# Measured durations in the forecast that orders the attention's matmuls, and token-reordering copies that run in the order of what they write

## The chip, the cores and the metric

The kernel runs on one core of a Trainium2 chip. The metric is the device time of one execution in microseconds (us), lower is better. Five engines matter here: TensorE (PE in the profile, with PEld for its weight loads), VectorE (DVE), ScalarE (ACT), GpSimd (POOL), and SyncE (SP), which issues most of the DMAs.

## The reference, cut to what matters

Two encoder layers on 512 tokens of width 1024, all in float32. Each layer has two token mixers that share one input projection, then an output projection, a normalisation and an MLP.

```python
for i in range(DEPTH):                                  # DEPTH = 2
    proj = x @ w_in[i]                                  # q, k, v of both mixers and the branch gates
    # mixer A: 8 query heads on 2 key/value heads, |i-j| <= 128, with a sink logit
    oa = banded_attention(rope(qa), rope(ka), va, 128, sink)
    # mixer B: three head groups, (window, dilation) = (128,1), (512,4), (2048,16)
    for g, (window, dil) in enumerate(B_GROUPS):
        outs[g], lse[g] = dilated_attention(rope(qb), rope(kb), vb, window, dil)
    ob = sum(softmax(lse, over groups) * outs)
    h = (sigmoid(gl_a) * (oa @ w_branch_a) + sigmoid(gl_b) * (ob @ w_branch_b)) @ w_out
    x = layer_norm(ALPHA * x + h)
    mlp = square(relu(x @ w_up)) @ w_down
    x = layer_norm(ALPHA * x + mlp + sigmoid(x @ w_ple_gate + b) * (p[i] @ w_ple))
```

## The kernel before, in words

Every float32 product is made of three passes of a rounded format: an operand is split into a high part (a cast on ACT, line 222) and a low part (source minus high part, on DVE, line 223), and TensorE adds high*high, high*low and low*high. Lines 274 to 276 are the three passes of a projection.

The attention of a layer is the part that the change touches. Its work on TensorE is of two kinds. The *filler* is the input projections (`ps_('qb', 0, 1)` and the like: 24 matmuls of 128x512, eight steps of three) and, at the end, the branch product `ya`. They need only the residual and the weights. The *units* are the attention proper: four of mixer A (`unit_a`, pairs of heads, names `sa`, `pta`, `oa`), six of mixer B (`unit_b`, names `sb`, `ptb`, `ob`) and two that combine mixer B's groups (`mix_b`, names `ex`, `ey`, `rs`). A unit of mixer A goes like this:

- scores of query block j into two banks (`sa_i_j`, line 433); DVE adds the mask and takes the maximum (line 426), a small DVE step makes the bias (`nm`, line 487), ACT makes the exponentials (line 422);
- transposes of the exponentials (`pta_i_n`, line 411, n from 0 to 5); ACT casts the high part (`ptha`), DVE subtracts for the low part (`ptla`);
- weighted sums of the values (`oa_i_r`, lines 437 and 438: line 437 needs `ptha`, line 438 needs `ptla`), three of these steps for each head r; ACT and DVE join the halves (lines 442, 443);
- a token scale: ACT widens the reciprocals (`wide`, line 450), TensorE transposes them (`rs`, line 456), DVE multiplies (line 457).

A projection of queries or keys is followed by the rotary step (`rope`): a shuffle on DVE (368), a product on DVE (369), a product on POOL (370), a sum on DVE (371), then the split into `qh` and `ql`. A projection of values is followed by a copy on ACT (`vTvb`, line 387 for dilated groups), transposes (`vtvb`, line 401) and a split (`vvvb`).

For the dilated groups the tokens are put in another order on the way. `natural` and `sigma` are two views of the 512 tokens of a row, with axes a (32), b (4), c (4); a token stands at 16a + 4b + c in the one and at 128c + 32b + a in the other.

The order on TensorE is set by a planner in the kernel. `Forecast` holds a clock `fc.t` of TensorE's time, books spans on ACT, DVE and POOL (`fc.on`), and knows when banks come free. At each turn the planner issues the next step of a live unit if the forecast says that its inputs are there, otherwise one step (three matmuls) of the filler, otherwise it lets 0.05 us of forecast time pass. Two limits hold the filler back: three banks for projections (`mm`), and five sets of queries and keys in use at a time (`held["qk"] - held["free_qk"] < 5`), where a unit gives its sets back when its last scores are issued. `HOP = 0.35` is the forecast's time from one engine to the next.

TensorE then runs in exactly that order (`manual_schedule(engines={PE})`). The order on the other engines is set by the scheduler of the framework, with its own estimates; the forecast does not set it. Weights are prepared two sets ahead: the cast `whi` (ACT, 1024 wide) and the subtraction `wlo` (DVE) of set c+2 take the buffer that set c-1 has left, and so start when a projection's last matmul but one is done.

Of the kernel before, what the change touches and what calls it, by code (L numbers as in the profile page):

```python
# [21 lines left out]
S = 512  # L22
# [177 lines left out]
def build(nc, tc, plan, down, xT, xN, pT, wst, vec, rows, sink, cst, out):  # L200
# [3 lines left out]
    with ctx:  # L204
# [138 lines left out]
        def attention_block(l, av, rp, vt, OA, OB, begun):  # L343
# [11 lines left out]
            def natural(ap):  # L355
                return ap.rearrange("p (a b c) -> p a b c", a=32, b=4)

            def sigma(ap):
                return ap.rearrange("p (c b a) -> p a b c", c=4, b=4)

            def forecast_split(n, after):
                h = fc.on("act", 0.05 + n / 1200, after + HOP)
                return h, fc.on("dve", 0.07 + n / 960, h + HOP)

            def rope(ps, dil, name):
                sw = av.tile([P, S], F32, tag="sw", name="sw" + name, bufs=2)
                t1 = av.tile([P, S], F32, tag="t1", name="t1" + name, bufs=2)
                nc.vector.stream_shuffle(sw, ps, SWAP)
                nc.vector.tensor_tensor(t1, ps, cc["cos"], ALU.mult)
                nc.gpsimd.tensor_tensor(sw, sw, cc["sin"], ALU.mult)  # L370
# [7 lines left out]
                a = fc.on("dve", 0.6, fc.t + HOP)  # L378
                b = fc.on("dve", 0.6, a)
                c = fc.on("pool", 1.23, a + HOP)  # L380
                fc.give("mm", b + HOP)
                return hi, lo, forecast_split(S, fc.on("dve", 0.6, max(b, c) + HOP))[1] + HOP

            def values(ps, kind, name):
                v = av.tile([P, S], F32, tag="vT", name="vT" + name, bufs=2)
                if kind == "sigma":
                    nc.scalar.copy(sigma(v), natural(ps))
# [6 lines left out]
                t = fc.on("act", 0.5, fc.t + HOP) + HOP  # L394
                fc.give("mm", t)
                return v, t

            def values_T(v, name):
                tp = bank("pt", "vt" + name)
                for b in range(4):  # L400
                    nc.tensor.transpose(tp[:, b * P:(b + 1) * P], v[:, b * P:(b + 1) * P], ident)
                vv = av.tile([P, 4, 2, 2, 64], F32R, tag="vv", name="vv" + name, bufs=3)
                split(vv[:, :, :, 0, :], vv[:, :, :, 1, :], tp.rearrange("p (b r d) -> p b r d", b=4, r=2))
                t = forecast_split(S, fc.pe(0.43))[1] + HOP
                fc.take("pt", t)
                return vv, t

            def probs_T(srcs, name):
                tp = bank("pt", "pt" + name)
                for i, s in enumerate(srcs):  # L410
                    nc.tensor.transpose(tp[:, i * P:(i + 1) * P], s, ident)  # L411
# [4 lines left out]
                t = forecast_split(n, fc.pe(n / 1200))[1] + HOP  # L416
                fc.take("pt", t)
                fc.take("pT")
                return hi, lo, t

            def exped(ap, bias, den, n, after):
                nc.scalar.activation(ap, ap, AF.Exp, bias=bias, scale=0.125, accum_out=den)
                return fc.on("act", 0.28 + n / 1200, after) + HOP

            def masked(dst, ps, mask, mx):
                nc.vector.tensor_tensor_reduce(dst, ps, mask, 1.0, NEG, ALU.add, ALU.max, mx)
                return fc.on("dve", 0.07 + mask.shape[-1] / 960, fc.t + HOP)
# [12 lines left out]
            def join(f, o, r):  # L440
                a, b = slice(r * 64, r * 64 + 64), slice(64 - r * 64, P - r * 64)
                nc.scalar.copy(f[a, :], o[b, :])
                nc.vector.tensor_tensor(f[a, :], o[a, :], f[a, :], ALU.add)
                t = fc.on("dve", 0.6, fc.on("act", 0.48, fc.t + HOP) + HOP) + HOP
                fc.give("o", t)
                return t

            def widened(c, name, after):
                wide = av.tile([P, 4, 2, 64], F32, tag="wide", name="wide" + name, bufs=1)
                nc.scalar.copy(wide, c.rearrange("p r (j u) -> p j r u", u=1).to_broadcast([P, 4, 2, 64]))  # L450
                return wide, fc.on("act", 0.52, after) + HOP

            def token_scaled(f, wide, name, after):
# [4 lines left out]
                t = fc.on("dve", 0.6, max(fc.pe(0.43) + HOP, after)) + HOP  # L458
# [7 lines left out]
            def unit_a(i):  # L466
# [9 lines left out]
                for j in range(4):  # L476
# [5 lines left out]
                    fc.pe(6 * w / 2400)  # L482
# [5 lines left out]
                    t = fc.on("dve", 0.08, t + 0.13) + HOP  # L488
# [7 lines left out]
                wide, t_wide = widened(den, nm_, ex[1, 3] + 0.6)  # L496
# [21 lines left out]
                for n, (r, kbs) in enumerate(groups):  # L518
# [8 lines left out]
                    for kb, p in zip(kbs, parts_of(n)):  # L527
                        w = len(p) * P
                        weighted(o[:, p[0][0] * P:p[0][0] * P + w], v, kb, r, pT, slice(c, c + w), kb == 0, kb == 2)
                        fc.pe(2 * w / 2400)  # L530
# [18 lines left out]
            def unit_b(sp, g, st):  # L549
# [4 lines left out]
                if g == 0:  # L554
# [6 lines left out]
                    for jj in range(2):  # L561
# [7 lines left out]
                        fc.pe(1.24)  # L569
# [10 lines left out]
                        t = fc.on("dve", 0.08, t + 0.13) + HOP  # L580
# [3 lines left out]
                else:  # L584
# [3 lines left out]
                    for c in range(4):  # L588
                        cs = slice(c * P, (c + 1) * P)
                        pair_scores(ss, q, k, cs, cs, cs)  # L590
                        fc.pe(0.64)
                    for s in range(2):
# [5 lines left out]
                        t = fc.on("dve", 0.08, t + 0.13) + HOP  # L598
# [27 lines left out]
                for n, (s, ms) in enumerate(groups):  # L626
# [7 lines left out]
                    if ms:  # L634
# [4 lines left out]
                        fc.pe(0.43)  # L639
                        if n % 2:  # L640
                            t_f = join(f, o, s)
                    else:
# [4 lines left out]
                        fc.pe(0.64)  # L647
                        nc.scalar.copy(natural(f[s * 64:s * 64 + 64, :]), sigma(o[:64, :]))
                        t_f = fc.on("act", 0.48, fc.t + HOP) + HOP
# [9 lines left out]
            def mix_b(sp, cn, cs):  # L659
# [11 lines left out]
                t1 = fc.on("dve", 0.6, fc.pe(0.43) + HOP) + HOP  # L671
# [23 lines left out]
                t += 2.6  # L695
# [38 lines left out]
            def steps(key, xs):  # L734
                yield lambda: fc.open("mm")
                w = weights(key)
                fc.on("dve", 1.135, fc.on("act", 0.947, fc.t + HOP) + HOP)
                ps = bank("mm", "ps_" + "_".join(str(v) for v in key))
                fc.take("mm")
                for i, x in enumerate(xs):  # L740
                    mm3(ps, w, i, x, i == 0, i == len(xs) - 1)
                    fc.pe(0.645)
                    yield None
                return ps

            def filler():
# [6 lines left out]
                for kind, *idx in FLOW:  # L753
# [9 lines left out]
                    elif kind == "g":  # L763
                        ps = yield from steps((l, ("g", 0, *idx)), X)
                        ga.append(gate(l, 0, idx[0], vt, rp, ps))
                        fc.give("mm", fc.on("act", 0.57, fc.t + HOP) + HOP)
                    else:
# [3 lines left out]
                        fc.on("dve", 1.135, fc.on("act", 0.947, fc.t + HOP) + HOP)  # L771
                        for n, g in enumerate(ga[2 * u:2 * u + 2]):
# [3 lines left out]
                            for i in range(4):  # L776
                                mm3(ps, w, n * 4 + i, OA[i], i == 0, i == 3)
                                fc.pe(0.645)
                                yield None
                            nc.vector.scalar_tensor_tensor(g, g, 1.0, ps, ALU.add, ALU.mult)  # L780
                            fc.give("mm", fc.on("dve", 0.6, fc.t + HOP) + HOP)
# [551 lines left out]
```

## Time and profile before

| | us |
|---|---|
| median of 3 runs | 1546.28 (1545.49 to 1547.36) |
| the profiled execution, time | 1546.11 |
| the profiled execution, span of its instructions | 1544.3 |
| attention of layer 1, from its first transposes to its last filler | 29.5 to 281.4 |
| attention of layer 2 | 798.0 to 1049.9 |

The profiled execution is 1.8 us longer than its span, and 0.17 us under the median. The mean granted clock of TensorE is 0.997. In the profile's rows a matmul's duration (0.39 us for 128x512) is longer than the step from one to the next (0.23 us), because they are pipelined; the step is what counts. The same holds in part on DVE and ACT: the next instruction starts some 0.05 to 0.1 us before the end that is shown.

### The profile page before, as it was taken

The page shows a single profiled execution, that of the slowest core. Times are in us where ns is not written, and L with a number is a line of the kernel's source. Part 1 is how long each engine was busy: PE and PEld are TensorE (multiplying, and loading weights), DVE is VectorE, ACT ScalarE, POOL GpSimd, SP SyncE. Part 2 cuts the span into 40 slices and gives each one's busy share as a digit, 9 for nine tenths or more (in the row PEclk, how much of TensorE's full clock was granted, in tenths as well). Part 3 has the DMA queues.
Part 4 walks back from the last instruction along what each step waited for, and adds up shares of the span by engine and source line. Part 5 has one row for each costly group of instructions (what it writes and reads, how often), then busy time and mean ns, then how long its engine had stood idle before and what let it go on. Part 6 is the DMA issues. An engine that isn't in the chain of part 4 may idle for free.

```text
span 1544.3 us, 19518 instructions
## 1 busy us (share of the span) xinstructions
PE 1512.5 (98%) x7416; PEld 1241.6 (80%) x7416; DVE 1091.1 (71%) x1809; ACT 714.9 (46%) x1186; POOL 201.3 (13%) x159
## 2 busy tenths in 40 slices
PE   8999999999999999999999999999999999999996
PEld 6778788888888888888887778888888888888885
DVE  6778675457568767696877786744575776767868
ACT  4566554344334443444546665543442443444342
POOL 1111110020011120202010101111100211111021
PEclk9999999999999999999999999999999999999998
DMA  6211224245622415142342121255456233241403
GB/s 219 69 55 56 69 69 167 85 127 161 194 71 81 145 49 161 44 151 68 96 149 68 56 69 56 81 164 148 134 140 207 68 98 121 71 134 55 150 1 95
DMA packets 46317, 162.19 MB, mean 105 GB/s; under 512 B 5648, under 2 KB 5776, under 8 KB 46224
## 3 DMA queue, kind: packets, MB, share of 16 engines
q1 hardware_dynamic: 43200, 152.00, 30.7%
q0 software_dynamic: 2448, 8.91, 3.1%
q8 instruction: 58, 0.95, 0.3%
q14 instruction: 35, 0.29, 0.1%
q10 hardware_dynamic: 576, 0.04, 0.0%
HBM read 155.16 MB, written 4.19 MB: 103 GB/s over the span
## 4 chain that ended last, share of the span: by engine, by line
PE 89%; DVE 6%; ACT 2%; DMA 2%; issue 1%; SPq 0%; ACTq 0%; DVEq 0%
PE dn L1004 17%; PE ps_up L275 8%; PE ps_up L274 8%; PE ps_up L276 8%; PE wo L281 2%; PE wo L282 2%; PE wo L280 2%; PE pg L282 2%; PE pg L281 2%; PE pg L280 2%; DVE wlo L223 1%; PE sa L433 1%; PE sb L433 1%; PE pta L411 1%; PE ps_start L274 1%
## 5 line engine op out<-in xcount | busy, mean ns | idle before, releaser
L223 DVE TENSOR_TENSOR wlo<-wst,whi 128x1024 fp32r<-128x1024 f32 (+1 forms) x171 | 220.2, 1291 | 149.5 <-ACT whi L222 144.8
L222 ACT CAST whi<-wst 128x1024 fp32r<-128x1024 f32 (+1 forms) x171 | 175.5, 1026 | 295.2 <-PE ps_up L275 115.5
L274 PE MATMUL ps_up<-xhi,whi 128*128 128x512 f32 x512 | 199.2, 389 | 0.0
L275 PE MATMUL ps_up<-xlo,whi 128*128 128x512 f32 x512 | 199.2, 389 | 0.0
L276 PE MATMUL ps_up<-xhi,wlo 128*128 128x512 f32 x512 | 199.2, 389 | 0.0
L977 POOL TENSOR_TENSOR hr<-r 128x512 f32<-128x512 f32 x64 | 102.2, 1597 | 551.4 <-ACT r L969 531.0
L274 PEld LDWEIGHTS ps_up<-xhi,whi 128*128 128x128 f32 x512 | 96.1, 188 | 20.0
L276 PEld LDWEIGHTS ps_up<-xhi,wlo 128*128 128x128 f32 x512 | 96.1, 188 | 20.0
L275 PEld LDWEIGHTS ps_up<-xlo,whi 128*128 128x128 f32 x512 | 96.1, 188 | 19.9
L222 ACT CAST whi<-raw 128x1024 fp32r<-128x1024 f32 x56 | 58.0, 1052 | 97.0 <-PE ps_up L275 57.6
L222 ACT CAST dhi<-raw 128x1024 fp32r<-128x1024 f32 x56 | 58.7, 1052 | 81.9 <-PE dn L1004 60.0
L1023 DVE TENSOR_TENSOR y<-y,dn 128x512 f32<-128x512 f32 x96 | 65.1, 682 | 38.7 <-PE dn L1004 38.7
L957 DVE TENSOR_TENSOR raw<-raw,raw 128x1024 f32<-128x1024 f32 x64 | 86.4, 1349 | 0.2
L223 DVE TENSOR_TENSOR wlo<-raw,whi 128x1024 fp32r<-128x1024 f32 x56 | 68.2, 1221 | 14.1 <-ACT whi L222 14.1
L223 DVE TENSOR_TENSOR dlo<-raw,dhi 128x1024 fp32r<-128x1024 f32 x56 | 69.2, 1239 | 5.4 <-ACT dhi L222 5.2
L1004 PE MATMUL dn<-whi,smh 128*128 128x512 f32 x128 | 50.1, 394 | 0.7 <-DVE y L1023 0.7
L282 PE MATMUL pg<-bhi,xlo 128*128 128x512 f32 x128 | 49.9, 390 | 0.9 <-DVE xlo L901 0.9
L1004 PE MATMUL dn<-wlo,smh 128*128 128x512 f32 x128 | 50.6, 395 | 0.2
L1004 PE MATMUL dn<-whi,sml 128*128 128x512 f32 x128 | 49.9, 390 | 0.0
L280 PE MATMUL pg<-bhi,xhi 128*128 128x512 f32 x128 | 49.9, 390 | 0.0
L1004 PE MATMUL dn<-dhi,smh 128*128 128x512 f32 x128 | 49.9, 390 | 0.0
L1004 PE MATMUL dn<-dlo,smh 128*128 128x512 f32 x128 | 49.8, 389 | 0.0
(834 smaller groups left out, 3878.4 us busy)
## 6 DMA issues: line engine op xcount, KB each, us to landing
wst<-wst SPq DMA_DIRECT2D x187, 512.0 KB, 3.6
raw<-wst SPq DMA_DIRECT2D x64, 512.0 KB, 4.3
y<-rows POOLq DMA_DIRECT2D x14, 512.0 KB, 7.8
row<-rows SPq DMA_DIRECT2D x7, 512.0 KB, 9.4
wst<-wst SPq DMA_DIRECT2D x10, 256.0 KB, 3.6
xs<-xT SPq DMA_DIRECT2D x8, 256.0 KB, 5.0
y<-xN SPq DMA_DIRECT2D x4, 512.0 KB, 6.2
kept<-y SPq DMA_DIRECT2D x4, 512.0 KB, 2.8
```

The costliest lines, as they stand in the source:

```text
L222: nc.scalar.copy(hi, src)
L223: nc.vector.tensor_tensor(lo, src, hi.bitcast(F32), ALU.subtract)
L274: nc.tensor.matmul(ps, w[0][:, s], x[0], start=start, stop=False, skip_group_check=part)
L275: nc.tensor.matmul(ps, w[0][:, s], x[1], start=False, stop=False, skip_group_check=part)
L276: nc.tensor.matmul(ps, w[1][:, s], x[0], start=False, stop=stop, skip_group_check=part)
L280: nc.tensor.matmul(ps, x[0], w[0][:, c], start=start, stop=False)
L281: nc.tensor.matmul(ps, x[0], w[1][:, c], start=False, stop=False)
L282: nc.tensor.matmul(ps, x[1], w[0][:, c], start=False, stop=stop)
L957: nc.vector.tensor_tensor(to, to, other, ALU.add)
L977: nc.gpsimd.tensor_tensor(h.rearrange("p s t -> p (s t)"), r, r, ALU.mult)
L1004: nc.tensor.matmul(ps[s], a[:, k, tok], w[b][:, cols], start=first and not (k or m), stop=k == 3 and m == 2, skip_group_check=True)
L1023: return nc.vector.tensor_tensor(to, to, ps, ALU.subtract if n in (2, 4, 5) else ALU.add)
```

## The change

Two things, both in the attention.

First, the durations that the forecast books are changed, nearly all of them upwards: a cast from 0.05 + n/1200 to 0.19 + n/1300, a subtraction from 0.07 + n/960 to 0.15 + n/960, a mask-and-maximum from 0.07 + n/960 to 0.24 + n/960, an exponential from 0.28 to 0.48 + n/1200, the small bias step from 0.08 to 0.2, the preparation of weights from 0.947 and 1.135 to 1.05 and 1.42, a filler step on TensorE from 0.645 to 0.681. Scores of mixer A go from 6w/2400 to 0.35 + 6w/4800; those of mixer B's groups become cheaper (1.24 to 1.1, and 0.64 to 0.45 for each of four).

Second, the copies that put the tokens into the dilated order run through the axes as c, b, a, where they ran as a, b, c. What is written is the same; the writes now go up by one element, and the reads jump by 16 elements, where before the reads went up by one and the writes jumped by 128. This holds for `qh`, `ql` (SBUF to SBUF) and for `vTvb` (PSUM to SBUF).

```diff
-            def sigma(ap):
-                return ap.rearrange("p (c b a) -> p a b c", c=4, b=4)
+            def sigma(ap, order="a b c"):
+                return ap.rearrange(f"p (c b a) -> p {order}", c=4, b=4)
...
             def forecast_split(n, after):
-                h = fc.on("act", 0.05 + n / 1200, after + HOP)
-                return h, fc.on("dve", 0.07 + n / 960, h + HOP)
+                h = fc.on("act", 0.19 + n / 1300, after + HOP)
+                return h, fc.on("dve", 0.15 + n / 960, h + HOP)
...
                 if dil:
-                    split(sigma(hi), sigma(lo), natural(t1))
+                    split(sigma(hi, "c b a"), sigma(lo, "c b a"), natural(t1, "c b a"))
...
                 if kind == "sigma":
-                    nc.scalar.copy(sigma(v), natural(ps))
+                    nc.scalar.copy(sigma(v, "c b a"), natural(ps, "c b a"))
...
-                return fc.on("dve", 0.07 + mask.shape[-1] / 960, fc.t + HOP)
+                return fc.on("dve", 0.24 + mask.shape[-1] / 960, fc.t + HOP)
...
-                    fc.pe(6 * w / 2400)
+                    fc.pe(0.35 + 6 * w / 4800)
...
-                fc.on("dve", 1.135, fc.on("act", 0.947, fc.t + HOP) + HOP)
+                fc.on("dve", 1.42, fc.on("act", 1.05, fc.t + HOP) + HOP)
```

No instruction is added or removed: each engine has as many as before. What moves is the order. On TensorE the units come later against the filler; three places show it, all of layer 1 (layer 2 has the same). In the rows below, the name ahead of the arrow is what is written, the last number of a name is a buffer's.

**Place A**, TensorE, the first unit of mixer A, around the scores `sa_1_2` and the third weighted step of `oa_0_0` (the one that reads `ptha_0_2` and `ptla_0_2`). Before:

```order
L274 MATMUL ps_('qb', 0, 0)_617<-xhi,whi_426 128x512
L275 MATMUL ps_('qb', 0, 0)_617<-xlo,whi_426 128x512
L276 MATMUL ps_('qb', 0, 0)_617<-xhi,wlo_427 128x512
L433 MATMUL sa_1_2_0_621<-qhka_285,qhqa_1_307 128x384
L433 MATMUL sa_1_2_1_622<-qhka_285,qhqa_1_307 128x384
L433 MATMUL sa_1_2_0_621<-qlka_286,qhqa_1_307 128x384
L433 MATMUL sa_1_2_1_622<-qlka_286,qhqa_1_307 128x384
L433 MATMUL sa_1_2_0_621<-qhka_285,qlqa_1_308 128x384
L433 MATMUL sa_1_2_1_622<-qhka_285,qlqa_1_308 128x384
L437 MATMUL oa_0_0_585<-ptha_0_2_595,vvva_322 128x384
L438 MATMUL oa_0_0_585<-ptla_0_2_596,vvva_322 64x384
```

and in the change:

```order
L411 MATMUL pta_0_2_623<-ident,pa_0_0_379 128x128 x3
L433 MATMUL sa_1_2_0_641<-qhka_285,qhqa_1_307 128x384
L433 MATMUL sa_1_2_1_642<-qhka_285,qhqa_1_307 128x384
L433 MATMUL sa_1_2_0_641<-qlka_286,qhqa_1_307 128x384
L433 MATMUL sa_1_2_1_642<-qlka_286,qhqa_1_307 128x384
L433 MATMUL sa_1_2_0_641<-qhka_285,qlqa_1_308 128x384
L433 MATMUL sa_1_2_1_642<-qhka_285,qlqa_1_308 128x384
L437 MATMUL oa_0_0_618<-ptha_0_1_595,vvva_322 128x384
L438 MATMUL oa_0_0_618<-ptla_0_1_596,vvva_322 64x384
L411 MATMUL pta_0_3_656<-ident,pa_0_1_380 128x128 x4
L437 MATMUL oa_0_0_618<-ptha_0_2_627,vvva_322 128x384
```

The projection `ps_('qb', 0, 0)` has moved ahead: it now ends just before this stretch (before, 18 more of its matmuls came behind it), and the next projection is held by the limit on query and key sets until `sa_1_3`. From there to `sa_1_3` no filler stands between the unit's steps.

On DVE the same stretch reads, before:

```order
L426 ISA pa_1_1_408,mxa_1_409<-sa_1_1_1_573,ct_142 128x384
L426 ISA mxa_1_409 128x1
L223 TENSOR_TENSOR wlo_614<-wst_611,whi_613 128x1024
L487 SCALAR_TENSOR_TENSOR nma_1_410<-mxa_1_409,nsk_145 128x2
L223 TENSOR_TENSOR ptla_0_2_595<-pta_0_2_590,ptha_0_2_594 128x384
L223 TENSOR_TENSOR ptla_0_3_606<-pta_0_3_600,ptha_0_3_605 128x512
```

and in the change:

```order
L426 ISA pa_1_1_414,mxa_1_415<-sa_1_1_1_603,ct_142 128x384
L426 ISA mxa_1_415 128x1
L368 STREAM_SHUFFLE sw_qb_0_631<-ps_('qb', 0, 0)_550 128x512
L369 TENSOR_TENSOR t_qb_0_632<-ps_('qb', 0, 0)_550,ct_142 128x512
L223 TENSOR_TENSOR wlo_700<-wst_697,whi_699 128x1024
L487 SCALAR_TENSOR_TENSOR nma_1_416<-mxa_1_415,nsk_145 128x2
L223 TENSOR_TENSOR ptla_0_2_628<-pta_0_2_623,ptha_0_2_627 128x384
```

The rotary step's shuffle and product have come in ahead of `ptla_0_2`, behind the mask step of `sa_1_1`.

**Place B**, TensorE, the third unit of mixer A against the scores `sa_3_2` and `sa_3_3`. Before:

```order
L276 MATMUL ps_('qb', 0, 1)_1020<-xhi,wlo_796 128x512
L437 MATMUL oa_2_0_1054<-ptha_2_1_1044,vvva_322 128x384
L438 MATMUL oa_2_0_1054<-ptla_2_1_1045,vvva_322 64x384
L411 MATMUL pta_2_3_1088<-ident,pa_2_1_747 128x128 x4
L274 MATMUL ps_('qb', 0, 1)_1020<-xhi,whi_795 128x512
L275 MATMUL ps_('qb', 0, 1)_1020<-xlo,whi_795 128x512
L276 MATMUL ps_('qb', 0, 1)_1020<-xhi,wlo_796 128x512
L437 MATMUL oa_2_0_1054<-ptha_2_2_1063,vvva_322 128x384
L438 MATMUL oa_2_0_1054<-ptla_2_2_1064,vvva_322 64x384
L411 MATMUL pta_2_4_1104<-ident,pa_2_1_747 128x128 x3
```

and in the change:

```order
L433 MATMUL sa_3_2_1_1090<-qhka_285,ql_qa_475 128x384
L437 MATMUL oa_2_0_1066<-ptha_2_1_1062,vvva_322 128x384
L438 MATMUL oa_2_0_1066<-ptla_2_1_1063,vvva_322 64x384
L411 MATMUL pta_2_3_1104<-ident,pa_2_1_762 128x128 x4
L437 MATMUL oa_2_0_1066<-ptha_2_2_1075,vvva_322 128x384
L438 MATMUL oa_2_0_1066<-ptla_2_2_1076,vvva_322 64x384
L411 MATMUL pta_2_4_1117<-ident,pa_2_1_762 128x128 x3
```

Here too the projection `ps_('qb', 0, 1)`, which stood in steps of three between the unit's steps, has moved ahead in one piece of 15 matmuls, and the next one is held until `sa_3_3`. On DVE the rotary step of `qb_1` and the subtraction of the next weights now stand ahead of `ptla_2_1`.

**Place V**, TensorE, the transposes of the values of mixer B's second group. Before, the projection's last step, nine matmuls of the next one, and then `vtvb`:

```order
L276 MATMUL ps_('vb', 0, 1)_1216<-xhi,wlo_1017 128x512
L274 MATMUL ps_('qb', 0, 2)_1359<-xhi,whi_1147 128x512
L275 MATMUL ps_('qb', 0, 2)_1359<-xlo,whi_1147 128x512
L276 MATMUL ps_('qb', 0, 2)_1359<-xhi,wlo_1148 128x512
L274 MATMUL ps_('qb', 0, 2)_1359<-xhi,whi_1147 128x512
L275 MATMUL ps_('qb', 0, 2)_1359<-xlo,whi_1147 128x512
L276 MATMUL ps_('qb', 0, 2)_1359<-xhi,wlo_1148 128x512
L274 MATMUL ps_('qb', 0, 2)_1359<-xhi,whi_1147 128x512
L275 MATMUL ps_('qb', 0, 2)_1359<-xlo,whi_1147 128x512
L276 MATMUL ps_('qb', 0, 2)_1359<-xhi,wlo_1148 128x512
L401 MATMUL vtvb_0_1_1369<-ident,vTvb_0_1_1351 128x128 x4
```

and in the change:

```order
L276 MATMUL ps_('vb', 0, 1)_1216<-xhi,wlo_977 128x512
L274 MATMUL ps_('qb', 0, 2)_1304<-xhi,whi_1147 128x512
L275 MATMUL ps_('qb', 0, 2)_1304<-xlo,whi_1147 128x512
L276 MATMUL ps_('qb', 0, 2)_1304<-xhi,wlo_1148 128x512
L274 MATMUL ps_('qb', 0, 2)_1304<-xhi,whi_1147 128x512
L275 MATMUL ps_('qb', 0, 2)_1304<-xlo,whi_1147 128x512
L276 MATMUL ps_('qb', 0, 2)_1304<-xhi,wlo_1148 128x512
L401 MATMUL vtvb_0_1_1311<-ident,vTvb_0_1_1296 128x128 x4
```

The transposes have come three matmuls nearer to the projection whose values they turn. The same six matmuls stand ahead of `vtvb_1_2`, where before there were three and 24 score matmuls. On ACT, in both kernels, the cast `whi` of the next weights stands ahead of the copy `vTvb`.

More of the change, by code (lines that the diff above doesn't have):

```diff
@@ L393, in values @@
                     nc.scalar.copy(v, ps)
-                t = fc.on("act", 0.5, fc.t + HOP) + HOP
+                t = fc.on("act", 0.9 if kind == "edge" else 0.6, fc.t + HOP) + HOP
                 fc.give("mm", t)
@@ L450, in widened @@
                 nc.scalar.copy(wide, c.rearrange("p r (j u) -> p j r u", u=1).to_broadcast([P, 4, 2, 64]))
-                return wide, fc.on("act", 0.52, after) + HOP
+                return wide, fc.on("act", 0.62, after) + HOP
             def token_scaled(f, wide, name, after):
@@ L457, in token_scaled @@
                 nc.vector.tensor_tensor(f, f, R, ALU.mult)
-                t = fc.on("dve", 0.6, max(fc.pe(0.43) + HOP, after)) + HOP
+                t = fc.on("dve", 0.69, max(fc.pe(0.49) + HOP, after)) + HOP
                 fc.take("pt", t)
@@ L495, in unit_a @@
                 nc.vector.reciprocal(den, den)
-                wide, t_wide = widened(den, nm_, ex[1, 3] + 0.6)
+                wide, t_wide = widened(den, nm_, ex[1, 3] + 2.1)
                 yield lambda: "va" in held
@@ L741, in steps @@
                     mm3(ps, w, i, x, i == 0, i == len(xs) - 1)
[L742 removed]
+                    fc.pe(0.681)
                     yield None
```

50 lines of the change are left out of this document (25 added, 25 removed).

## Prediction, on record before the changed kernel ran

> **What bounds the kernel now.** I read the page first (busy times, then the chain that ended last), then the list of what TensorE waited for, then the timeline at each of those waits.
>
> ```profile
> span 1544.3 us, 19518 instructions
> ...
> PE 1512.5 (98%) x7416; PEld 1241.6 (80%) x7416; DVE 1091.1 (71%) x1809; ACT 714.9 (46%) x1186; POOL 201.3 (13%) x159
> ...
> PE 89%; DVE 6%; ACT 2%; DMA 2%; issue 1%; SPq 0%; ACTq 0%; DVEq 0%
> ```
>
> TensorE is busy for 98% of the span and carries 89% of the chain. The change adds and removes no matmul, so it can only gain what TensorE waits for in the two attentions, and a little at the seams between kinds of matmuls. This is what it waits for, but for one wait of 0.9 outside the attention:
>
> ```profile
> PE ps_start L274 <- ACT whi L222: 5.7, 1, 5.7
> PE vtvb L401 <- ACT vTvb L387: 3.1, 2, 1.5
> PE pta L411 <- ACT pa L422: 2.2, 4, 0.7
> PE ob L438 <- DVE ptlb L223: 1.6, 2, 0.8
> PE dn L1004 <- DVE y L1023: 1.5, 4, 0.4
> PE rs L456 <- ACT wide L450: 1.5, 4, 0.4
> PE ob L646 <- DVE ogb L443: 1.4, 2, 0.7
> ```
>
> `ps_start` and `dn` lie outside the attention. The other five make 3.1 + 2.2 + 1.6 + 1.5 + 1.4 = 9.8 us in 14 waits, seven in each layer. A wait costs more than is listed, since the pipeline runs dry:
>
> ```profile
> 127.94 0.39 PE L275 MATMUL ps_('qb', 0, 2)_1359<-xlo,whi 128*128 128x512 f32 x1
> 128.17 0.39 PE L276 MATMUL ps_('qb', 0, 2)_1359<-xhi,wlo 128*128 128x512 f32 x1
> 130.09 0.66 PE L401 MATMUL vtvb<-ident,vTvb 128*128 128x128 f32 x4 [1.53 <-ACT vTvb L387]
> ```
>
> The usual step is 0.23 (127.94 to 128.17); here it is 1.92, so 1.69 are lost where 1.53 are listed, 0.16 more. With 14 x 0.16 = 2.2 the attentions lose 12.0 us, 6.0 in each layer. That is the most that a better order can win by waits.
>
> **The change, part by part: the old waits.** I counted in the order what TensorE has to do between the work that a wait depends on and the place where it waits, before and in the change, with the steps quoted further down. The wait for the first exponentials had 2.8 us of such work and was 0.8 short; it now has 4.9. The second one goes from 4.0 (0.6 short) to 6.0. The bank of `ob_0_1`: from 2.0 (0.9 short) to 4.7. `ob_1_0` behind its transposes: from 2.3 (1.0 short) to 4.1. The last widened weights: from 4.8 (0.6 short) to 6.8. All these have more work than they lacked, so I take them as gone. The first widened weights have 7.4 us as before (0.4 short); following DVE's and ACT's new order there, the weights are ready about 1 us ahead, so I count this gone too, and keep 0.4 per layer for the range. That leaves `vtvb`, whose work shrinks.
>
> **Place V, and the copies.** What the copy waits for:
>
> ```profile
> 229.81 0.39 PE L276 MATMUL ps_('vb', 1, 2)_2386<-xhi,wlo 128*128 128x512 f32 x1
> 230.06 1.06 ACT L222 CAST whi<-wst 128x1024 fp32r<-128x1024 f32 x1 [0.25 <-PE ps_('vb', 1, 2)_2386 L275]
> 231.02 1.08 ACT L387 COPY vTvb<-ps_('vb', 1, 2)_2386 128x512 f32<-128x512 f32 x1
> ```
>
> and, earlier in the layer, the copy that the wait above stands on:
>
> ```profile
> 129.00 1.05 ACT L387 COPY vTvb<-ps_('vb', 0, 1)_1216 128x512 f32<-128x512 f32 x1
> ```
>
> The cast of the next weights goes first; call E the end of the projection's last step (229.81 + 0.23 = 230.04). The copy starts at E + 0.98. How long it takes when its writes are in order, no row shows for this line. The nearest are:
>
> ```profile
> L442 ACT COPY fa<-oa 64x512 f32<-64x512 f32 x8 | 4.7, 582 | 1.4 <-PE oa L438 1.2
> L648 ACT COPY ogb<-ob 64x512 f32<-64x512 f32 x8 | 4.6, 580 | 7.1 <-PE ob L646 6.9
> ```
>
> Both read PSUM and write in order; L442 reads in order too, L648 reads with jumps of 128 elements. They take the same, 582 and 580 ns. So the ends are 0.58 and the 1.08 of now, and I take 0.58, because L648 is the same engine, source and kind of read. The values are then there at E + 0.98 + 0.58 + 0.04 = E + 1.60 (0.04 is from the end of the copy at 129.00 + 1.05 to TensorE's 130.09). TensorE arrives after six matmuls, at E + 1.36. Lost: 0.24, at two places per layer (`vtvb_0_1`, `vtvb_1_2`), 0.5 per layer.
>
> [...]
>
> For `qh` and `ql` the source is in SBUF, which no row shows with jumps in the reads. The ends are the plain and the reordered duration of now:
>
> ```profile
> L222 ACT CAST qh_kb<-t_kb x6: 616/1120/1139, 82.3 to 228.7; 128x512 fp32r<-128x512 f32 x6
> ```
>
> 0.62 and 1.12. Either way no wait hangs on it: scores of a dilated group come 8 us or more of TensorE's work behind the keys' projection, against 6.2 at the least before with no wait listed. Cost nothing, both ends.
>
> **Places A and B.** Here the units run without filler between their steps, so TensorE goes at the pace of DVE. TensorE's steps:
>
> ```profile
> 100.82 0.28 PE L437 MATMUL oa<-ptha,vvva 128*128 128x256 f32 x1
> ...
> 101.29 0.49 PE L411 MATMUL pta<-ident,pa 128*128 128x128 f32 x3
> 101.54 0.47 PE L274 MATMUL ps_('qb', 0, 1)_1020<-xhi,whi 128*128 128x512 f32 x1
> ...
> 102.41 0.44 PE L433 MATMUL sa<-qhka,qh_qa 64*128 64x384 f32 x2
> ...
> 103.13 0.50 PE L274 MATMUL ps_('qb', 0, 1)_1020<-xhi,whi 128*128 128x512 f32 x1
> ...
> 103.93 0.34 PE L437 MATMUL oa<-ptha,vvva 128*128 128x384 f32 x1
> ...
> 104.28 0.60 PE L411 MATMUL pta<-ident,pa 128*128 128x128 f32 x4
> 104.64 0.47 PE L274 MATMUL ps_('qb', 0, 1)_1020<-xhi,whi 128*128 128x512 f32 x1
> ```
>
> Scores of 384 take 0.72, a weighted step 0.47 (256, twice) or 0.35 (384), three transposes 0.25, four 0.36; three filler matmuls behind another kind about 0.8. DVE's steps:
>
> ```profile
> 58.93 0.56 DVE L426 CUSTOM_DVE_ANT_0 pa<-sa,ct 128x384 f32<-128x384 f32 x1 [1.29 <-PE sa L433]
> ...
> 59.89 1.22 DVE L223 TENSOR_TENSOR wlo<-wst,whi 128x1024 fp32r<-128x1024 f32 x1
> 61.03 0.15 DVE L487 SCALAR_TENSOR_TENSOR nma<-mxa,nsk 128x2 f32<-128x2 f32 x1
> 61.10 1.15 DVE L223 TENSOR_TENSOR ptla<-pta,ptha 128x384 fp32r<-128x384 f32 x2
> 62.17 0.55 DVE L426 CUSTOM_DVE_ANT_0 pa<-sa,ct 128x384 f32<-128x384 f32 x1
> ...
> 69.73 0.74 DVE L368 STREAM_SHUFFLE sw_qb<-ps_('qb', 0, 0)_617 128x512 f32<-128x512 f32 x1
> 70.36 0.67 DVE L369 TENSOR_TENSOR t_qb<-ps_('qb', 0, 0)_617,ct 128x512 f32<-128x512 f32 x1
> ```
>
> Two mask steps 0.96 (58.93 to 59.89), `wlo` 1.14, bias 0.07, a subtraction of 384 0.5, shuffle 0.63, product 0.6. And while POOL does the rotary product, DVE stands:
>
> ```profile
> 225.45 0.67 DVE L369 TENSOR_TENSOR t_kb<-ps_('kb', 1, 2)_2317,ct 128x512 f32<-128x512 f32 x1
> 225.69 1.29 POOL L370 TENSOR_TENSOR sw_kb<-sw_kb,ct 128x512 f32<-128x512 f32 x1 [6.36 <-DVE sw_kb L368]
> 226.04 2.03 DVE L223 TENSOR_TENSOR wlo<-wst,whi 128x1024 fp32r<-128x1024 f32 x1
> ```
>
> `wlo`, started 0.94 before POOL ends (226.98), takes 2.03 and ends at 228.07, 1.09 behind POOL.
>
> A: let 0 be the start of `pta_0_0`. TensorE without waits: seven transposes to 0.6, filler 1.4, `sa_1_1` 2.1, the last filler 2.9, weighted 3.4, `pta_0_2` and the turn to scores 3.8, `sa_1_2` 4.5, weighted 4.9, `pta_0_3` 5.3, and line 438 of the third weighted step at 5.5. DVE has `sa_1_1` at 2.3: masks and one subtraction 1.44, to 3.8; shuffle 4.4; product 5.0; POOL from 4.7 to 6.0; `wlo` to 7.1; bias and `ptla_0_2` to 7.6. TensorE waits 2.1. Then the masks of `sa_1_2` to 8.6, while TensorE reaches `sa_1_3` at 8.3: 0.3 more. A costs 2.4.
>
> B: let 0 be the end of `ps_('qb', 0, 1)`. TensorE: `pta_2_1`, weighted, `pta_2_2`, `sa_3_2`, and line 438 at 0.25 + 0.47 + 0.4 + 0.72 + 0.35 = 2.2. DVE: shuffle from 0.2 to 0.8, POOL from 1.05 to 2.35, `wlo` to 3.4, `ptla_2_1` to 3.9. TensorE waits 1.7. What follows is in time.
>
> New waits per layer: 2.4 + 1.7 + 0.5 = 4.6, in place of 6.0. Two layers: -2.8 us.
>
> **Seams.** Per two layers the filler is left for another kind of work 126 times before and 124 times in the change; each costs about 0.2 (the first filler matmul behind another kind steps 0.1 longer, and so does the last ahead of scores). -0.4.
>
> **Sum.** 1546.11 - 2.8 - 0.4 = 1542.9, against the profiled execution, which stands 0.17 under the median.
>
> **The rivals.**
> *A and B are covered after all* (POOL's lock-out falls elsewhere, or DVE is further ahead): then V alone remains, 12.0 + 0.4 - 1.0 = 11.4 gained, 1534.7. Against it: the rotary step's place ahead of `ptla` is fixed by DVE's order, and its start by the projection's end.
> *The copies don't shorten.* V's values come at E + 2.1, 0.74 late instead of 0.24, at four places: 2.0 more, 1544.9. L648 speaks against it.
> *The change doesn't do what it says:* the waits move to other edges and add up to the old 12 us, 1546. Ten edges per layer in A and B have less work than any of their kind had before; I followed those that come first.
> *Slower: the hops.* My walks take 0.04 to 0.2 from one engine to the next. If a hop cost the 0.35 that the forecast books, some eight hops in each of A and B add about 2 us each, 4.1 per layer: 1542.9 + 8.2 = 1551. It decides from 3.2 more per layer, a hop 0.2 longer than I read. The 0.04 at 130.09 speaks against it.
>
> **How the numbers follow.** Forecast 0.54, covered 0.12, copies 0.11, moved elsewhere 0.15, hops 0.08. What a measurement can tell from no change is 0.2%, 3.1 us. The forecast's own range, by an error of 1 us in each of A and B and 0.4 for the widened weights, is 1538.5 to 1546; it is faster than 1543.2 in somewhat over half. Faster: 0.12 + 0.33 + 0.03 of the copies = 0.48; slower 0.08; same 0.44. The range from 1537.5 to 1547.5 leaves out most of "covered" and of "hops".
>
> **What would show it.** Waits of `vtvb` short, of `pta`, `ob` and `rs` gone; new ones of `oa` line 438 on `ptla` of about 2 us, twice a layer, with `wlo` of 2 us on DVE ahead; `vTvb` at 0.58. Wrong, if `oa` does not wait, or other pairs lose 4 us.

## The result: slower by 0.55%, and the profile after

| | us |
|---|---|
| the change, median of 4 runs | 1555.38 (1552.74 to 1557.1) |
| the kernel before, 4 runs on the same chip | 1546.57 (1545.49 to 1547.36) |
| ratio | 1.0055, 95% interval 1.0043 to 1.0068 |
| predicted | 1542.9 (1537.5 to 1547.5) |
| the profiled execution, time and span | 1556.71 and 1554.9 |

The first line of the page, and the list of what TensorE waited for (us in total, times, longest):

```profile
span 1554.9 us, 19514 instructions
...
PE oa L438 <- DVE ptla L223: 6.7, 4, 1.8
PE ps_start L274 <- ACT whi L222: 5.1, 1, 5.1
PE vtvb L401 <- ACT vTvb L387: 4.2, 2, 2.1
PE ptb L411 <- DVE ptlb L223: 3.5, 2, 1.7
PE dn L1004 <- DVE y L1023: 1.7, 5, 0.4
PE rs L456 <- DVE ptlb L223: 0.5, 2, 0.2
```

The old waits of `pta` and `ob` are gone, and so is that of the first `rs` for its widened weights: the `rs` in this list is a later one, and it waits for the low part `ptlb`. In their place stand fewer and longer ones. Per layer, as steps of TensorE beyond the usual step (both layers agree within 0.04):

| place | time in layer 1 | predicted | lost |
|---|---|---|---|
| A, `oa_0_0` line 438 | 66.35 | 2.4 | 1.93 |
| B, `oa_2_0` line 438 | 108.31 | 1.7 | 1.76 |
| V, `vtvb_0_1` | 128.81 | 0.24 | **2.24** |
| `oa` line 438, later | 149.01 | 0 | 0.28 |
| P, `ptb_0_1_0` | 160.26 | 0 | **1.90** |
| the second `rs` | 207.41 | 0 | 0.38 |
| V, `vtvb_1_2` | 236.07 | 0.24 | 0.24 |
| sum | | 4.6 | 8.73 |

Two layers lose 17.5 by waits where the kernel before loses 12.0: 5.5 more, not 2.8 less. The rest is in the table of stretches (length; busy times; then PEclk, the granted TensorE clock; DMA share; GB/s):

```profile
core 0: us, PE busy (x) PEld busy (x) DVE busy (x) ACT busy (x) POOL busy (x), PEclk, DMA share, GB/s
...
69.80:72.60 2.80, 2.80 (x10) 2.19 (x9) 2.80 (x10) 2.37 (x7) 0.00 (x0) 0.50 0.31 119
...
881.70:884.20 2.50, 2.50 (x10) 1.97 (x10) 2.39 (x8) 0.99 (x2) 0.00 (x0) 0.50 0.66 211
...
906.00:908.80 2.80, 2.80 (x10) 2.32 (x9) 1.88 (x11) 1.36 (x5) 0.00 (x0) 0.50 0.53 178
```

Behind A in layer 1, and behind B and V in layer 2, the clock was halved: a matmul of 512 columns stepped 0.427 instead of 0.227. The windows above are cut out of three slow stretches; in the trace's record of the granted clock each of them lasts 3.41 us (from 69.24, from 881.61 and from 905.51). What they cost is read from the same matmuls in the other layer, where the clock was whole. From the end of the wait to the first matmuls at full speed it took 4.39 against 2.99 behind A, 3.87 against 2.33 behind B and 5.12 against 3.59 behind V: 1.40 + 1.54 + 1.53 = 4.5 us.

Waits and clock together make 5.5 + 4.5 = 10.0. The trace shows 9.55: the same matmul of the filler starts 0.42 later than before ahead of the first attention (47.85 against 47.43), 4.33 later behind it (268.02 against 263.69), 4.60 later ahead of the second (820.57 against 815.97) and 10.25 later behind it (1042.42 against 1032.17), so 3.9 + 5.65 for the two. Some 0.4 was gained elsewhere in the two attentions.

The record also shows which waits drew a slow stretch. In the profile of the change the times at which the granted clock changes lie whole multiples of 3.41 us apart (881.61 and 905.51 are 238 and 245 of them behind 69.24), so time is read here in cells of 3.41 us. Five cells of the change that hold a long wait, and the slow cell behind the first (length; busy time of TensorE with its matmuls; granted clock; DMA share; GB/s):

```profile
65.83:69.24 3.41, 1.64 (x12) 1.00 0.15 19
69.24:72.65 3.41, 3.41 (x12) 0.50 0.34 135
106.79:110.20 3.41, 1.97 (x15) 1.00 0.00 0
127.27:130.68 3.41, 1.93 (x9) 1.00 0.03 7
878.20:881.61 3.41, 1.83 (x14) 1.00 0.00 0
902.10:905.51 3.41, 1.42 (x16) 1.00 0.00 0
```

The three slow stretches begin at the ends of the three cells in which TensorE stood longest: 1.77 (A, layer 1), 1.58 (B, layer 2) and 1.99 (V, layer 2). B and V in layer 1 come next with 1.44 and 1.48, and kept the clock. A wait that falls across the border of two cells leaves less idle time in each: A left 1.77 in one cell in layer 1 and 1.17 at most in layer 2, B 1.44 and 1.58, V 1.48 and 1.99, and the same wait drew a slow stretch in one layer and not in the other.

Place A went as the prediction walked it (POOL, DVE and TensorE):

```profile
65.58 1.28 POOL L370 TENSOR_TENSOR sw_qb<-sw_qb,ct 128x512 f32<-128x512 f32 x1 [14.43 <-DVE sw_qb L368]
...
65.92 2.02 DVE L223 TENSOR_TENSOR wlo<-wst,whi 128x1024 fp32r<-128x1024 f32 x1
...
67.94 0.55 DVE L223 TENSOR_TENSOR ptla<-pta,ptha 128x384 fp32r<-128x384 f32 x1
...
68.54 0.39 PE L438 MATMUL oa<-ptla,vvva 128*64 128x384 f32 x1 [1.77 <-DVE ptla L223]
```

Place B went the same way:

```profile
107.47 1.28 POOL L370 TENSOR_TENSOR sw_qb<-sw_qb,ct 128x512 f32<-128x512 f32 x1 [23.66 <-DVE sw_qb L368]
...
107.81 2.02 DVE L223 TENSOR_TENSOR wlo<-wst,whi 128x1024 fp32r<-128x1024 f32 x1
...
110.35 0.39 PE L438 MATMUL oa<-ptla,vvva 128*64 128x384 f32 x1 [1.60 <-DVE ptla L223]
```

Place V did not go as the prediction walked it. ACT's rows, then TensorE's:

```profile
127.84 0.45 ACT L422 ACTIVATE pb<-pb,cn 128x192 f32<-128x192 f32 x1
...
129.63 0.19 ACT L422 ACTIVATION_READ_ACCUMULATOR pb<-pb,cn 128x1 f32 x1
129.72 1.03 ACT L222 CAST whi<-wst 128x1024 fp32r<-128x1024 f32 x1
130.66 0.57 ACT L387 COPY vTvb<-ps_('vb', 0, 1)_1216 128x512 f32<-128x512 f32 x1
...
128.81 0.39 PE L276 MATMUL ps_('qb', 0, 2)_1304<-xhi,wlo 128*128 128x512 f32 x1
131.28 0.66 PE L401 MATMUL vtvb<-ident,vTvb 128*128 128x128 f32 x4 [2.08 <-ACT vTvb L387]
```

The copy takes 0.57, but four exponentials run from 127.84 to 129.72 ahead of the cast and the copy; in the kernel before they ran behind the copy, from 129.82. Place P, which the prediction did not walk:

```profile
158.86 0.19 ACT L422 ACTIVATION_READ_ACCUMULATOR pb<-pb,cs 128x1 f32 x1
158.96 0.56 ACT L387 COPY vTvb<-ps_('vb', 0, 2)_1458 128x512 f32<-128x512 f32 x1
159.42 1.05 ACT L222 CAST whi<-wst 128x1024 fp32r<-128x1024 f32 x1
160.37 0.58 ACT L222 CAST pthb<-ptb 128x512 fp32r<-128x512 f32 x1
...
160.50 1.23 DVE L223 TENSOR_TENSOR wlo<-wst,whi 128x1024 fp32r<-128x1024 f32 x1 [4.56 <-ACT whi L222]
161.65 0.69 DVE L223 TENSOR_TENSOR ptlb<-ptb,pthb 128x512 fp32r<-128x512 f32 x1
...
162.39 0.66 PE L411 MATMUL ptb<-ident,pb 128*128 128x128 f32 x4 [1.74 <-DVE ptlb L223]
```

The bank that `ptb_0_1_0` needs is free when `ptlb_0_0_2` is done; ahead of it stand `pthb`, `whi`, the value copy, and eight exponentials of `sb_0_1`, which ended when the copy began at 158.96.

### The profile page after: what moved, and what is told of

Its sections match the earlier page's. It is cut to its first block, busy times and chain, and to the rows that moved or that the text cites. A ratio compares the mean times of both kernels' runs of the same rounds, so it can differ in the third digit from the quotient of the medians.

```text
span 1554.9 us, 19514 instructions
## 1 busy us (share of the span) xinstructions
PE 1518.9 (98%) x7416; PEld 1245.3 (80%) x7416; DVE 1092.6 (70%) x1809; ACT 712.7 (46%) x1186; POOL 196.9 (13%) x159
## 4 chain that ended last, share of the span: by engine, by line
PE 86%; DVE 8%; ACT 3%; issue 2%; DMA 1%; SPq 0%; ACTq 0%; DVEq 0%
PE dn L1004 15%; PE ps_up L275 7%; PE ps_up L274 7%; PE ps_up L276 7%; PE pg L282 2%; PE wo L281 2%; PE wo L280 2%; PE wo L282 2%; PE pg L280 2%; PE pg L281 2%; PE sa L433 1%; DVE wlo L223 1%; PE ps_start L274 1%; PE ps_start L275 1%; PE ya L274 1%
## 5 line engine op out<-in xcount | busy, mean ns | idle before, releaser
L223 DVE TENSOR_TENSOR wlo<-wst,whi 128x1024 fp32r<-128x1024 f32 (+1 forms) x171 | 227.5, 1333 | 168.7 <-ACT whi L222 167.7
```

Source lines behind the costliest of these rows:

```text
L223: nc.vector.tensor_tensor(lo, src, hi.bitcast(F32), ALU.subtract)
```

## The experiments

Theories: *waits* (ACT's and DVE's orders make the long waits), *clock* (TensorE slows behind them), and as rivals that the copies lose the time, or that TensorE's order is short of work whatever the other engines do. Where an experiment changes the order on ACT or DVE, it names an instruction that has to be issued before another; TensorE's order stays that of the change, row for row. In kernels with added lines the line numbers below are a few higher than in the kernel shown. Ratios are against the kernel before, run alongside on the same chip; the numbers in brackets are the 95% interval.

**The forecast alone.** The new durations, with the old copies:

```diff
-                    split(sigma(hi, "c b a"), sigma(lo, "c b a"), natural(t1, "c b a"))
+                    split(sigma(hi), sigma(lo), natural(t1))
-                    nc.scalar.copy(sigma(v, "c b a"), natural(ps, "c b a"))
+                    nc.scalar.copy(sigma(v), natural(ps))
```

> The new durations in the forecast, with the old copies. TensorE's order is that of the changed kernel row for row, and so are the other engines' orders. Theory of the waits (what the change lost are waits of TensorE that its new order makes): the order is what loses, and the slower copy makes it worse, since it stands ahead of the waits of vtvb (two places) and of ptb: 0.5 us more at each, 1.5 per layer, so 1555.4 + 3 = 1558.4 us. Rival, the copies lose the time (reads that jump, or contention from them): most of the 9 us is gone, 1546 to 1549.

Measured: 1560.39 (1558.62 to 1565.81), ratio 1.0094 [1.0081, 1.0108]. The waits:

```profile
PE oa L438 <- DVE ptla L223: 7.2, 6, 1.8
PE vtvb L401 <- ACT vTvb L387: 6.2, 4, 2.5
...
PE ptb L411 <- DVE ptlb L223: 4.5, 2, 2.2
```

The order loses the time, and the longest waits of `vtvb` and `ptb` are each 0.5 longer, as the slower copy says. The time is 5.0 over the change's, where 3 were expected. In the profiled executions the two attentions together take 2.8 more, at mean granted clocks that are near each other (0.994 and the change's 0.993), so the waits account for what was expected; the rest was not followed up.

**The copies alone.** The reverse: `natural`, `sigma` and the two lines as in the change, the durations as before.

> The new copies with the old forecast. The orders are those of the kernel before. Theory of the waits: the value copy takes 0.57 us instead of 1.08, so the wait of vtvb_0_1 falls from 1.69 lost to about 1.2, once per layer, and nothing else changes: 1546.6 - 1.0 = 1545.6. Rival, the copies lose: 1550 or more. If the cast and the subtraction in the other direction (1.09 and 1.05 instead of 1.12 and 1.15) matter anywhere, a little less than 1545.6.

Measured: 1544.76 (1543.75 to 1546.42), ratio 0.9991 [0.9982, 1.0000]. `vtvb` waits 0.7 less per layer (3.1 before):

```profile
PE vtvb L401 <- ACT vTvb L387: 1.7, 2, 0.9
```

The copies gain 1.75, at the edge of what this measurement can tell. They are not what lost the time.

**TensorE kept at work in the four long waits.** The line of the edit that makes the matmuls; it is called 7 or 8 times at each of the four places:

```diff
+                nc.tensor.matmul(ps, zero, X[0][0], start=False, stop=False, skip_group_check=True)
```

> The changed kernel, with TensorE kept at work in the four long waits of each layer (A, B, vtvb_0_1, ptb_0_1_0): 7 or 8 matmuls of 512 columns with zero weights, added to a bank that is being summed, fill 1.6 to 1.8 us of each wait. The waits' ends don't move, so by the waits alone the time is that of the change, 1552.7 to 1557.1 with the same spread. Theory of the clock (TensorE falls to steps of 0.43 us for 2 to 3 us behind some of the waits, because it stood still): those stretches are gone in both layers, and the time is about 1546.6 + 5.5 (waits) - 0.4 (seams) = 1551.7, with runs that lie within 2 us of each other.

Measured: 1553.1 (1552.65 to 1554.75), ratio 1.0044 [1.0032, 1.0057], 2.3 under the change. The table of stretches at A and behind it:

```profile
66.00:68.50 2.50, 2.50 (x14) 1.84 (x12) 2.50 (x4) 0.92 (x2) 0.97 (x1) 1.00 0.00 0
...
69.80:72.60 2.80, 2.80 (x17) 2.29 (x16) 2.80 (x10) 2.48 (x7) 0.00 (x0) 1.00 0.34 138
```

The waits end as late, and the clock is whole: 1.00 at A and behind it, and 0.997 in the mean, as in the kernel before, where the change had 0.993. So the stretches of the change came from standing still. From the first scores to the same filler matmul behind each attention, the profiled execution takes 1.4 and 3.1 less than the change's, 4.5 together, which is the cost read above; against the kernel before it takes 2.5 more in each, 5.0, near the 5.5 that the waits lose by the table. By the medians the gain is 2.3, less than the 3.7 expected, and the two intervals overlap, so it is the clock in the trace that settles this and not the time. That the runs lie closer (2.1 between the ends, 4.4 for the change) fits, but says little: the four runs with the longer hop, below, have the lowest mean granted clock of all (0.988 to 0.989) and lie within 0.6.

**Exponentials behind (ACT).** For V and P; `ahead_of_exps(x, set)` has x issued before the exponentials of the set, which are the four of `sb_0_0_0` (`exps0`) and the last four of `sb_0_1` (`exps1`):

```diff
+                    if name.endswith("_0_1"): ahead_of_exps(copy, "exps0")
+                    if name.endswith("_0_2"): ahead_of_exps(copy, "exps1")
...
+                if key[1] == ("g", 0, 3): ahead_of_exps(cast[0], "exps1")
...
+                if name == f"b{l}_0_0_2": ahead_of_exps(cast[0], "exps1")
```

> The changed kernel, TensorE's order untouched; on ACT alone, four exponentials of sb_0_0_0 go behind the cast whi and the copy vTvb_0_1, and four exponentials of sb_0_1 go behind the copy vTvb_0_2, the cast whi and pthb_0_0_2. Theory of the waits, that ACT's order makes the two waits which the prediction missed: vtvb_0_1 falls from 2.24 lost to about 0.35, ptb_0_1_0 from 1.90 to about 0.2, 3.6 per layer, and with two long waits fewer about 1.5 less at the slow clock: 1555.4 - 7.2 - 1.5 = 1546.7. Rival, that the places are short of work on TensorE in any order of ACT: the same work ends at the same time, and the time stays at 1553 to 1557.

Measured: 1551.21 (1548.79 to 1554.1), ratio 1.0031 [1.0020, 1.0042]. `vtvb_0_1` lost 0.39 and `ptb_0_1_0` 0.34, where 2.24 and 1.90 had been lost:

```profile
PE vtvb L405 <- ACT vTvb L389: 0.5, 2, 0.2
...
PE ptb L415 <- DVE ptlb L225: 0.4, 2, 0.2
```

A new loss came, 0.84 of waiting and 1.08 with the steps around it, one step later on TensorE, since the copy on ACT that frees the bank `ob` now stood behind the four exponentials:

```profile
158.97 0.58 ACT L452 COPY ogb<-ob 64x512 f32<-64x512 f32 x1
...
160.32 0.38 PE L447 MATMUL ob<-pthb,vvvb 128*128 128x256 f32 x1 [0.84 <-DVE ogb L453]
```

So 2.5 per layer were won instead of 3.6, and the mean granted clock of its profile was 0.995, between the change's 0.993 and the 0.997 of the kernel before, so slow stretches were still in its trace. ACT's order is shown to be the cause of V and P; the time was missed by 4.5, through the new loss and the stretches that stayed.

**`wlo` behind (DVE).** For A and B; `low[0]` is the `wlo` just asked for, `("low", i, n)` is `ptla_i_n`, and `("last", i, j)` the second mask of `sa_i_j`:

```diff
+                for x in {("kb", 0, 0): [("low", 0, 2), ("last", 1, 2)],
+                          ("kb", 0, 1): [("low", 2, 1), ("low", 2, 2), ("last", 3, 2)]}.get(key[1], []):
+                    tc.add_manual_dep(low[0].ins, held[x].ins.name, ...)
```

> The changed kernel, TensorE's order untouched; on DVE alone, at places A and B the subtraction wlo (2.02 us there) goes behind the low parts ptla and the masks that TensorE waits for. Theory of the waits, that A and B are DVE's queue and nothing else: the losses of 1.93 and 1.76 per layer fall to 0.1 to 0.4 each, the two long waits per layer at vtvb_0_1 and ptb_0_1_0 stay: 1555.4 - 6.4 - about 1 at the slow clock = 1548. Rival, that the units run dry there anyway because no filler stands between their steps: the wait goes to the next step (the masks of sa_1_2, ptla_2_2) and 1 us or more per place stays, 1551 to 1553.

Measured: 1552.78 (1550.56 to 1552.9), ratio 1.0034 [1.0022, 1.0047]. B's loss is gone. At A 0.80 stayed and 0.97 came anew, for the join of `oa_0_0` that frees the bank:

```profile
PE oa L439 <- DVE fa L445: 1.6, 2, 0.8
...
PE oa L440 <- DVE ptla L225: 1.3, 2, 0.6
```

The theory was right at B. At A the rival was nearly right: the wait went to the next steps, and the time lies in the range that the rival gave.

**All four at once**: the edits of the last two, with the copy of `ob_0_0_0` ahead of the exponentials too.

> All four places at once: DVE's order as in the run before, ACT's as in the run that put exponentials behind, and the copy of ob_0_0_0 ahead of the four exponentials too (there TensorE had waited 0.84 for that bank). TensorE's order is that of the change. Theory of the waits and the clock: per layer 0.39 + 0.28 + 0.34 + 0.39 + 0.24 are left, with 0.3 for A and B about 2.0 instead of the 6.0 of the kernel before; no wait is over 1 us, so no stretch at the slow clock: 1546.5 - 8.0 - 0.4 = 1538.1, with runs within 2 us of each other. Rival, a change of order that brings waits of its own elsewhere: 1543 or more.

Measured: 1542.74 (1542.0 to 1543.63), ratio 0.9973 [0.9962, 0.9985]. TensorE runs the order of the change, and is 12.6 faster than the change. Per layer 3.4 are lost by waits, 1.75 of them at A, against 6.0 before; the mean granted clock is 0.996 in the profiled execution and 0.997 in the other six, as in the runs of the kernel before, and the runs lie within 1.6. So with TensorE's order held fixed, other orders on ACT and DVE take away the whole loss of the change and more. Of the 4.6 over what was expected, A is 2.9 (1.75 instead of 0.3 per layer); the rest was not followed up. What is left at A is in DVE's rows, first place A and then B, each with POOL's product:

```profile
66.03 1.28 POOL L372 TENSOR_TENSOR sw_qb<-sw_qb,ct 128x512 f32<-128x512 f32 x1 [14.44 <-DVE sw_qb L370]
106.43 1.28 POOL L372 TENSOR_TENSOR sw_qb<-sw_qb,ct 128x512 f32<-128x512 f32 x1 [23.66 <-DVE sw_qb L370]
...
66.37 0.96 DVE L499 SCALAR_TENSOR_TENSOR nma<-mxa,nsk 128x2 f32<-128x2 f32 x1
...
106.77 1.01 DVE L225 TENSOR_TENSOR ptla<-pta,ptha 128x384 fp32r<-128x384 f32 x2
```

A step on two numbers takes 0.96 at A, up to POOL's end; two subtractions of 384 take 1.01 together at B, beside POOL.

**Place A mended.**

```diff
+                    if (i, n) == (0, 2) and ("bias", 1, 1) in held:
+                        tc.add_manual_dep(held["bias", 1, 1].ins, low[0].ins.name, ...)
-                for x in {("kb", 0, 0): [("low", 0, 2), ("last", 1, 2)],
+                for x in {("kb", 0, 0): [("low", 0, 3), ("add", 0, 0)],
```

> The kernel with all four places mended, and place A mended further on DVE: there the bias step of two numbers had taken 0.96 us behind POOL's product (0.15 elsewhere), ahead of ptla_0_2, while two subtractions with one operand in PSUM ran at 0.50 each under POOL's product at place B. So ptla_0_2 goes ahead of the bias, and wlo behind ptla_0_3 and the join of oa_0_0. Theory, that only DVE steps with both operands in SBUF wait for POOL: ptla_0_2 runs at 0.5 under POOL's product, the losses of 0.78 and 0.97 per layer at A fall to 0.3 in all, 1542.7 - 2.9 = 1539.8. Rival, that whatever DVE runs first there waits for POOL, two places at B being chance: ptla_0_2 takes 1.0 or more, the 0.78 stay, and only the second wait goes: 1541.

Measured: 1539.75 (1539.06 to 1541.16), ratio 0.9957 [0.9944, 0.9971]: the fastest kernel here.

```profile
65.33 1.28 POOL L372 TENSOR_TENSOR sw_qb<-sw_qb,ct 128x512 f32<-128x512 f32 x1 [14.46 <-DVE sw_qb L370]
...
65.67 0.55 DVE L225 TENSOR_TENSOR ptla<-pta,ptha 128x384 fp32r<-128x384 f32 x1
66.13 0.50 DVE L499 SCALAR_TENSOR_TENSOR nma<-mxa,nsk 128x2 f32<-128x2 f32 x1
```

`ptla` runs beside POOL in 0.55, and the bias again waits for POOL's end. The losses at A fell to 0.20 + 0.18 + 0.54 per layer, more than the 0.3 in all that was expected. That the time came out at the 1539.8 expected is luck in part: from the first scores to the filler behind, the two attentions are 1.7 shorter in all than in the run with all four places, and the rest of the 3.0 between the two medians does not come from them.

**A more careful forecast.** First a longer hop (`HOP = 0.6`), then value transposes 1.5 us later (`fc.t >= t + 1.5`):

> The changed kernel with HOP = 0.6 instead of 0.35 in the forecast: every step of a unit is asked for 0.25 us later. The theory says that a more careful forecast does not help by itself, since DVE's and ACT's orders, which make the waits, are not what it forecasts: other places, the same kind of waits, 1546 to 1558. If more slack is what the order lacks: 1540 or less.

> The changed kernel where the transposes of values (va, vtvb) are asked for 1.5 us later than their forecast, nothing else. vtvb is needed late, so the delay is free. At the place V the wait should go (2.2 per layer); but the planner then sets all that follows anew, so A, B and P move too. Theory as for the longer hop: 1544 to 1556, with vtvb without a wait; if vtvb alone were the loss, 1550.

Measured: 1565.01 (1564.9 to 1565.5), ratio 1.0118 [1.0105, 1.0132], and 1560.5 (1558.11 to 1564.18), ratio 1.0091 [1.0077, 1.0104]: both outside what was expected, both slower than the change. With the longer hop a wait that the change doesn't have leads, and the mean granted clock is 0.988:

```profile
PE sa L433 <- DVE mxa L426: 13.3, 8, 3.1
```

With the late transposes `vtvb` is not in the list of waits any more, and `oa`, `sa` and `pta` wait in its place. In these two kernels slack in the forecast moved the waits and did not lower them; why the two orders are worse was not taken apart.

## Why the prediction was wrong, point by point

- *The old waits go*: right, that of the first `rs` too. It starts at 197.99 a usual 0.20 behind the matmul ahead of it; its widened weights were ready at 197.48, 0.5 ahead where I had 1. The 0.38 in the table is the second `rs` of the same unit, at 208.02, whose weights had been ready since 199.35. It waits for the bank that `ptlb` frees, an edge that the prediction did not follow.
- *The copy at 0.58*: right; the eight copies take 0.56 to 0.59:

```profile
L387 ACT COPY vTvb<-ps_('vb', 0, 1)_1216 x1: 572/572/572, 130.7 to 130.7; 128x512 f32<-128x512 f32 x1
...
L222 ACT CAST qh_kb<-t_kb x12: 621/1092/1117, 86.1 to 1007.2; 128x512 fp32r<-128x512 f32 x12
```

  The cast `qh` from SBUF did not shorten (1.09 against 1.12), nor did `ql` by much (1.05 against 1.15): the upper end of the bounds. No wait hung on it, as said.
- *Place V* is the first step that failed, for `vtvb_0_1`: 2.24 lost instead of 0.24. The step was "the cast of the next weights goes first ... the copy starts at E + 0.98". That is ACT's order in the kernel before; in the change the cast still goes ahead of the copy, but other work goes ahead of both. With E = 127.45 + 0.23 = 127.68, TensorE arrived at E + 1.36 as said, but the copy started at E + 2.98: four exponentials had moved there. `vtvb_1_2`, where ACT's order did not change, lost the 0.24 of the sum to the hundredth. ACT's new order could have been read beforehand, as DVE's was for A and B.
- *Places A and B*: the mechanism and nearly the size (1.93 and 1.76 for 2.4 and 1.7). The 0.3 at `sa_1_3` did not come. The slower rival, hops of 0.35, was wrong: it would have made A and B longer.
- *"I followed those that come first"* is the second step that failed: P, 1.90 per layer, lies on an edge I left out; there too ACT's exponentials stood ahead. The rival "the waits move to other edges" was the right family, and its 1546 too low, since it took the old sum as the bound of the new. The prediction's own sign of being wrong, other pairs that lose 4 us, came: V and P lose 7.8 more than the sum had for them.
- *The clock* was in no term: 4.5 us of the profiled execution's loss, about 2.3 of the median's. A sum of waits alone gives 1546.1 + 5.5 = 1551.6.
- *The seams*, -0.4: neither shown nor refuted. Waits and clock make 10.0 where the trace has 9.55, and with the waits filled the attentions lose 5.0 where the waits make 5.5. So about 0.4 was gained somewhere, and no run says that it was at the seams.
- *The range*: an error of 1 us in each of A and B makes 4.0 over two layers, and 0.4 for the widened weights makes 0.8, so these errors reach from 1538.9 to 1547.7, not from 1538.5 to 1546. The measured time lies outside either way.

## What to carry to other kernels

A planner that sets one engine's order cannot be judged on its own forecast alone: here the waits were made by the order on the engine that feeds TensorE, and ACT's and DVE's orders were set elsewhere. With TensorE's order held fixed, some dozen instructions per layer put in another place on those two engines moved the time from 1555.4 to 1539.75; the forecast with measured durations was slower than the old one, and the two more careful ones were slower still. Before costing a wait in a new order, read what stands ahead of the feeding instruction on its own engine in the new order, at every edge that lost work, and look at the granted clock behind each long wait: here three TensorE waits of 1.60 to 2.08 cost 1.40 to 1.54 again in clock, and five others of 1.60 to 2.08 did not.

## What the runs showed of the hardware

- TensorE's granted clock fell to 0.50 behind some waits that were shorter than the stretch it then stayed slow (3.41 in the change; longer with the late transposes, 0.50 from 843.3 to 849.0): behind 3 of 8 waits of 1.60 to 2.08 in the change, and not behind the two of 1.53 and 1.52 in the profile of the kernel before; in the profile with the waits filled the mean was 0.997 (0.993 in the change). With the late transposes it fell once behind a wait of 0.45 and before the end of one of 1.03, which ended 1.75 later, so it is not the length of one wait that decides. The same wait at the same place drew it in one layer and not in the other. In the attentions of the change and of the kernel before it went by the idle time within one cell of 3.41: the slow stretches stand behind the three cells with 1.58, 1.77 and 1.99, while the cells of the change with 1.48 and less kept the clock, and so did one with 1.52 in the kernel before. This is not the whole condition: with the late transposes a cell with about 1.15 lost it. What decides besides the idle time of a cell stays open.
- While POOL multiplied two SBUF tiles (1.28), a DVE step with both operands in SBUF lasted to POOL's end, however small (0.96 and 0.50 for two numbers, 0.15 elsewhere), or past it (`wlo` 2.02 for 1.23, to 1.08 behind POOL's end at A), and a DVE step with one operand in PSUM did not (`ptla` 0.50 to 0.55). Once per layer of the kernel before it went the other way: `wlo` took its 1.22 (at 109.97) and POOL's product 2.76.
- Of the copies that reorder, ACT read PSUM in jumps of 16 elements as fast as a copy that reads in order (`vTvb` 0.57 against 0.58 at L442), and SBUF not (the cast `qh` 1.09 against 0.62).
